# One gate pair moved from behind the attention into the head, attention scores and turned weights in separate PSUM places, and three more places for FFN rows

## The chip, the core and the metric

The kernel runs on one core of one Trainium2 chip. The metric is the device time of one execution in microseconds; the time before is the median of three runs, 1458.77 us (1458.38 to 1460.04). The core's engines are TensorE (PE; its weight loads are shown apart as PEld), VectorE (DVE), ScalarE (ACT), GpSimd (POOL) and SyncE (SP). Here POOL and SP mostly issue DMAs, and POOL does a few copies and memsets.

## The reference

One layer of a streaming encoder, over 1024 frames of a new stream and 64 frames of a running one; all in float32, with D_MODEL 1024, 8 heads of 64, CONV_DIM 512, D_FF 2816:

```python
def mixer(xn, conv_prefix, attn_fn, w_in, w_conv, w_conv_out, w_attn_out, w_out):
    proj = xn @ w_in
    cb, cc, ch, q, k, v, ga, gb = jnp.split(proj, splits, axis=-1)
    cv, conv_state = causal_conv(cc * ch, conv_prefix, w_conv)
    ya = (cb * cv) @ w_conv_out
    o, new_k, new_v = attn_fn(heads(q), heads(k), heads(v))
    yb = o.reshape(B, L, ATT_DIM) @ w_attn_out
    merged = jax.nn.sigmoid(ga) * ya + jax.nn.sigmoid(gb) * yb
    return merged @ w_out, conv_state, new_k, new_v

def swiglu(x, w1, w3, w2):
    return (jax.nn.silu(x @ w1) * (x @ w3)) @ w2

x = x + mixer(rmsnorm(x, g_mix), ...)
x = x + swiglu(rmsnorm(x, g_ffn), w_ff1, w_ff3, w_ff2)
return rmsnorm(x, g_final)
```

The attention is banded: a frame sees its own chunk of 64 and the eight before it, with a learned bias by clipped distance. `ga` and `gb` are 1024 channels each, the two gates.

## The kernel before

**Numbers.** Every product is made of three matmuls: a float32 operand is split into a high part (a cast on ACT) and a low part (a subtraction on DVE; `split`, lines 128 and 129), and high x high, high x low and low x high are added up in PSUM. Columns are the 1088 frames, in two halves of 544 (HT), each in two pieces of 272 (HN).

**The head.** Most columns of w_in go through `Unit` and `run`, one unit for 256 output channels: a 2 x 2 Strassen scheme with seven products instead of eight, each of 4 blocks x 3 matmuls x 2 pieces = 24 matmuls of 272 columns (line 280). `units` (line 540) is the order: q, k, cc, ch, cb, three of ga, and then four ya units (the product with w_conv_out, half as deep: 12 matmuls a product). A ga unit takes the sigmoid and stores its rows in DRAM (`a_done`); `gated_load` loads the rows of unit u into free parts of the scratch tile while an earlier unit runs, and `ya_done` multiplies them into the ya rows and stores these in `y_d`. The fourth ya unit has no gate unit in the head and stores its rows bare. The forms of the ya operand are written by `uforms` during the last unit ahead of ya.

**The gates outside the head.** Gates are 128-channel rows. The eight gb rows and the two ga rows 6 and 7 are plain products (`product`, lines 346 to 348): 4 pieces, each of 8 blocks x 3 = 24 matmuls. `plan` is the order of their weights, `prep` loads and splits them ahead, `next_w` hands them out; four pairs fit. The `x21` loads bring back the quarter of the normalised input whose place the Strassen forms took, which the pieces 2 and 3 of each gate need.

**The attention.** `attention` is a generator with 75 turns for 8 heads x 9 query tiles (t = 0 to 7 of the prompt with 1 to 5 key blocks of 128, and t = 8 for the sample): scores of step i, `softmax` (DVE adds the bias and takes the maximum, ACT takes exp and the sum), the transposes of step i - 2 with a `split` of the turned weights out of PSUM, and the value product of each pair of tiles one step later. Scores and turned weights share the PSUM pool `patt`, two buffers of two banks each, one tag. With the gates' three banks (`pmm`) and one for values (`ppv`) that is all eight banks. `between` lets PER = 3.15 turns run after each gate piece. The order: pieces 0 and 1 of four gates, then their pieces 2 and 3 and the other gates with attention turns behind each piece; ahead of the last LAST = 2 gates (ga 6 and 7) the attention is finished, and the tiles for the merge are made. The tile framework fixes the order on each engine when the program is built, by priority (order in the code) and by its own idea of when operands are ready.

**The merge.** For each row m in MERGE the yb product (lines 346 to 348, in `psum2`), z = sigmoid(gb) and t = the ya row are merged by DVE. `rows_in` loads gb and ya rows from DRAM. Rows 6 and 7 of ya are multiplied by their ga rows first (line 1189).

**The FFN.** The up products of 256 hidden channels are again Strassen units, (`a`, `b`) for w_ff1 and w_ff3. `hidden_done` forms seven combinations of a hidden row's halves and `keep` splits each into a row place and stores it in `h_d` (POOL, line 1458). There are three places: one in `hp` (hq) and two in `early` (hq_early). From the third pair on, part of the products is made jointly; `joint_forms` prepares operands for it in three tiles tj5, tj6, tj7 (first as tw6, tw7) of the pool `l2p`. The down product ends the kernel.

Of the kernel before, what the change touches and what calls it, by code (L numbers as in the profile page):

```python
# [8 lines left out]
F32 = mybir.dt.float32  # L9
# [6 lines left out]
P = 128  # L16
# [19 lines left out]
C_CB, C_CC, C_CH, C_Q, C_K, C_V, C_GA, C_GB = 0, 512, 1024, 1536, 2048, 2560, 3072, 4096  # L36
PER = 3.15
LAST = 2
# [28 lines left out]
def encoder_kernel(ctx: ExitStack, tc: tile.TileContext, ins, outs):  # L67
# [265 lines left out]
    def next_w():  # L333
        i = used[0]
        used[0] += 1
        prep(4 if i == 3 else i + 2)
        return plan[i]
# [13 lines left out]
    MERGE = [6, 7, 0, 1, 2, 3, 4, 5]  # L351
    GATES = [("b", m) for m in MERGE] + [("a", m) for m in range(6, 8)]
    for g, m in GATES:
        if m % 2 == 0:
            base = (C_GA if g == "a" else C_GB) + m * P
            ld = {"src": w_in[:, base : base + 2 * P], "w": 2 * P}
        plan.append((ld, KD, m % 2 * P))
# [183 lines left out]
    for nm, u in (  # L541
        ("q", 0), ("q", 1), ("k", 0), ("k", 1), ("cc", 0), ("ch", 0), ("ga", 0), ("cb", 0), ("cc", 1), ("ch", 1),
        ("ga", 1), ("cb", 1), ("ga", 2),
    ):
        base = {"q": C_Q, "k": C_K, "cc": C_CC, "ch": C_CH, "cb": C_CB, "ga": C_GA}[nm]
        units.append((nm, u, w_in[:, base + 2 * u * P : base + 2 * (u + 1) * P]))
# [167 lines left out]
    def ya_done(u):  # L714
        def f(r, h, src, snap):
            if u == 3:
                s = summed(src, snap, "ya")
            else:
                g = gated.pop((u, r, h))
                if snap is None:  # L720
                    s = snap1(None, "ya")
                    two = [t.rearrange("p (j n) -> p j n", j=2) for t in (s, g)]
                    vec.tensor_tensor(two[0], src, two[1], op=ALU.mult)
                else:
                    s = summed(src, snap)
                    vec.tensor_tensor(s, s, g, op=ALU.mult)
            nc.gpsimd.dma_start(row_of(y_d, u, r, h), s)

        return f
# [114 lines left out]
    for n in range(len(units)):  # L844
# [8 lines left out]
        else:  # L853
# [10 lines left out]
            unit = nxt_unit  # L864
        if n >= 12 and n < 15:
            gated_load(n - 12)
        if n == 13:
            x21_load(2)
        if n == 14:
            plain_load(0)  # L870
        for _ in r:
            if n == 12:
                uforms(si)
            if n < 2 and si in (2 + n, 5 + n):
                i = 2 * n + si // 5
                cache_tile(i)
                if i + 2 < 4:
                    cache_load(i + 2)
            if si > 1:
                for f in due:  # L880
                    f()
                due.clear()
            due += late
            late.clear()
            si += 1
# [15 lines left out]
    def gate(i, cs):  # L901
        g, m = GATES[i]
        for c in cs:
# [3 lines left out]
            if i >= len(GATES) - LAST:  # L907
                gate_out[0] = act.activation(ga_rows[m - 6][:, o : o + n], ps[:, :n], AF.Sigmoid).ins
                continue
# [89 lines left out]
    def scores(h, t):  # L999
        q, k, ks, v, vs, bias = heads[h]  # L1000
        ps = patt.tile([P, 2, 512], F32, tag="att", name=f"s{h}_{t}")
        s = at_pool.tile([P, 640], F32, tag="s", name=f"p{h}_{t}", bufs=4)
# [25 lines left out]
    def transposed(h, t, s):  # L1028
        tp = patt.tile([P, 2, 512], F32, tag="att", name=f"t{h}_{t}").rearrange("p a b -> p (a b)")
        if t == 8:  # L1030
            pt = pts_one
            for i in range(4):
                nc.tensor.transpose(
                    tp[:, i * TS : (i + 1) * TS], s[:TS, i * P : (i + 1) * P], ident[:TS, :TS]
                )
            nc.tensor.transpose(tp[:TS, 512 : 512 + TS], s[:TS, 512:576], ident[:TS, :TS])
            split(pt[:, 0, :4, :], pt[:, 1, :4, :], tp[:, : 4 * TS].rearrange("p (b t) -> p b t", t=TS))
            split(pt[:TS, 0, 4, :], pt[:TS, 1, 4, :], tp[:TS, 512 : 512 + TS])
            pts[h, 4] = pt

            sm = sums.pop(h)
            vec.reciprocal(sm, sm)
            tr = patt.tile([P, 2, 512], F32, tag="att", name=f"rt{h}")[:9, 0, :P]
            nc.tensor.transpose(tr, sm, ident)
# [14 lines left out]
        b0 = t - nb + 1 - max(0, 2 * g - 4)  # L1059
        for i in range(nb):  # L1060
            nc.tensor.transpose(tp[:, i * P : (i + 1) * P], s[:, i * P : (i + 1) * P], ident)  # L1061
        src = tp[:, : nb * P].rearrange("p (b t) -> p b t", t=P)
        js = slice(j * P, (j + 1) * P)
        split(pt[:, 0, b0 : b0 + nb, js], pt[:, 1, b0 : b0 + nb, js], src)

# [77 lines left out]
    def rows_in(m):  # L1143
        t, z = rows[m] = u_rows.tile([P, T], F32, tag="yg", name=f"yg{m}"), row_tile((MERGE.index(m) % 5 + 1) % 2, f"gb{m}")
        nc.sync.dma_start(z, gb_d[m * P : (m + 1) * P])
        nc.sync.dma_start(t, y_d[m * P : (m + 1) * P])
# [3 lines left out]
    x21_load(0)  # L1150
    for i in range(4):
        gate_w[i] = next_w()
        gate(i, (0, 1))
    for i in range(4):
        for c in (2, 3):
            gate(i, (c,))
            between()
        if i == 0:
            prep(5)
    for i in range(4, len(GATES)):  # L1160
        gate_w[i] = next_w()
        if i == len(GATES) - LAST:
# [7 lines left out]
            u_rows = pg_stack.enter_context(tc.tile_pool(name="u_rows", bufs=5, reuse_waits="tile"))  # L1170
            ga_rows = [uo.tile([P, T], F32, name=f"ga{m}") for m in (6, 7)]
            for k in range(2):
# [10 lines left out]
        for c in range(4):  # L1183
            gate(i, (c,))
            between()
        if i >= len(GATES) - LAST:
            m = GATES[i][1]
            t = rows[m][0]
            vec.tensor_tensor(t, t, ga_rows[m - 6], op=ALU.mult)


# [4 lines left out]
    for n, m in enumerate(MERGE):  # L1196
# [3 lines left out]
        t, z = rows.pop(m)  # L1200
        with tc.issue_after(gate_out[0]):
            act.activation(z, z, AF.Sigmoid)
        late = t.rearrange("p (h n) -> p h n", h=2)[:, :, 512:]
# [236 lines left out]
    def hidden_done(p):  # L1440
# [4 lines left out]
        def keep(c, x):  # L1445
# [3 lines left out]
            else:  # L1449
                n, kept_rows[0] = kept_rows[0] % 3, kept_rows[0] + 1  # L1450
                if n:
                    if kept_rows[1] is None:
                        kept_rows[1] = early.tile([P, 2, 4, 2, P], F32R, tag="raw", name="hq_early")
                    hq = kept_rows[1][:, n - 1]
                else:
                    hq = hp.tile([P, 4, 2, P], F32R, tag="hq", name=f"hq{p}_{c}", bufs=1)
# [206 lines left out]
    with tc.issue_after(urgent[0]), tc.issue_after(urgent[1]):  # L1663
# [4 lines left out]
        wp_stack.close()  # L1668
        hp = ctx.enter_context(tc.tile_pool(name="hp", bufs=2, reuse_waits="tile"))
    with tc.issue_after(newest[0]):  # L1670
        next(r0)
# [28 lines left out]
    def joint_forms():  # L1700
        l2p = up_stack.enter_context(tc.tile_pool(name="l2p", bufs=1, reuse_waits="tile"))

        def at(q, dtype, nm):
            return l2p.tile([P, 2, 2, HN], dtype, tag=f"tj{q}", name=nm)

# [422 lines left out]
```

## Time and profile before

| | us |
|---|---|
| median of three runs | 1458.77 (1458.38 to 1460.04) |
| the profiled execution | 1459.0 |
| its span, first to last instruction | 1456.9 |
| TensorE's granted clock, mean | 0.998 |

The page gives the busy time of each engine over the span; matmuls overlap and their ends are modelled, so the distance of one matmul's start from the next says more than the busy share. The stages by time: 0 to 66 norm and values of the head, 66 to 344 the Strassen units, 344 to 385 ya, 385 to 412 gate pieces alone, 412 to 590 the attention, 590 to 611 the last gates, 611 to 659 yb and merge, then the output product and the second norm, the FFN's up products from 787 on, the down product from about 1220 to the end.

### The profile page before, as it was taken

To read this page: it belongs to the slowest core of one execution; us is meant where nothing else is said; L and a number is where in the kernel's file an instruction comes from. 1 tells how busy PE (TensorE), PEld (TensorE's weight loads), DVE (VectorE), ACT (ScalarE), POOL (GpSimd) and SP (SyncE) were. 2 spreads that over 40 slices of the span, in tenths; PEclk is the share of its full clock that TensorE was granted. 3 is DMA by queue.
4 is the path that set the end of the run, shared out by engine and by line. 5 is a ranking of instruction groups with operands and counts; after the bars stand their busy time and mean duration, and the time that the engine had idled before them with its cause. 6 is when DMAs were issued, how large, how long until landed. Compare 5 with 4: busy or idle time off the path is not lost.

```text
span 1456.9 us, 26281 instructions
## 1 busy us (share of the span) xinstructions
PE 1441.3 (99%) x10083; PEld 1354.3 (93%) x10083; DVE 1033.4 (71%) x1939; ACT 693.3 (48%) x1389; POOL 156.2 (11%) x292
## 2 busy tenths in 40 slices
PE   8999999999999999999999999999999999999997
PEld 6899999999999989998889999999999998888886
DVE  7975565658457777572589787777777788857677
ACT  7654343436357667531456445454444455513223
POOL 1400010000211121111000111111011111000000
PEclk9999999999999999999999999999999999999999
DMA  8586512225878675843432444443344459767676
GB/s 284 184 281 224 192 63 74 66 102 198 251 218 213 171 191 149 294 150 117 152 112 75 155 169 144 155 149 130 136 143 162 164 201 324 251 230 246 214 266 208
DMA packets 156221, 262.48 MB, mean 180 GB/s; under 512 B 18528, under 2 KB 89376, under 8 KB 156096
## 3 DMA queue, kind: packets, MB, share of 16 engines
q1 hardware_dynamic: 132336, 184.33, 40.0%
q0 software_dynamic: 22608, 74.38, 14.2%
q10 hardware_dynamic: 1152, 2.10, 0.4%
q8 instruction: 79, 1.29, 0.4%
q14 instruction: 46, 0.38, 0.1%
HBM read 171.78 MB, written 90.81 MB: 180 GB/s over the span
## 4 chain that ended last, share of the span: by engine, by line
PE 87%; issue 8%; DVE 2%; ACT 1%; DMA 1%; POOL 1%; SPq 0%; ACTq 0%; POOLq 0%; DVEq 0%
PE A L2038 8%; PE Ab L1848 7%; PE Aa L1848 7%; PE D L2038 4%; PE Db L1848 4%; PE Da L1848 4%; PE J L1859 3%; PE g L347 3%; PE g L348 3%; PE g L346 3%; PE Aga L280 2%; PE B L2038 2%; PE t L1061 2%; PE Ak L280 2%; PE Aq L280 2%
## 5 line engine op out<-in xcount | busy, mean ns | idle before, releaser
L346 PE MATMUL g<-xn,wp 128*128 128x272 f32 x320 | 93.9, 294 | 0.0
L347 PE MATMUL g<-xn,wp 128*128 128x272 f32 x320 | 93.0, 291 | 0.0
L348 PE MATMUL g<-xn,low 128*128 128x272 f32 x320 | 92.9, 290 | 0.0
L128 ACT CAST ring<-w2r 128x512 fp32r<-128x512 f32 (+1 forms) x78 | 43.2, 587 | 96.0 <-PE A L2038 49.3
L972 DVE CUSTOM_DVE_ANT_0 p<-s,bb 128x640 f32<-128x640 f32 (+5 forms) x72 | 47.6, 662 | 38.5 <-PE s L1015 36.9
L2038 PE MATMUL A<-ring,low 128*128 128x512 f32 (+1 forms) x270 | 72.6, 384 | 0.0
L2038 PE MATMUL A<-ring,ht 128*128 128x512 f32 (+1 forms) x267 | 72.4, 387 | 0.0
L346 PEld LDWEIGHTS g<-xn,wp 128*128 128x128 f32 x320 | 60.3, 188 | 0.6
L347 PEld LDWEIGHTS g<-xn,wp 128*128 128x128 f32 x320 | 60.3, 188 | 0.4
L348 PEld LDWEIGHTS g<-xn,low 128*128 128x128 f32 x320 | 60.2, 188 | 0.4
L128 ACT CAST wa<-rawa 128x512 fp32r<-128x512 f32 x46 | 28.4, 621 | 66.2 <-PE Db L1848 20.9
L2038 PEld LDWEIGHTS A<-ring,low 128*128 128x128 f32 x270 | 50.1, 188 | 10.2 <-DVE acc L2053 0.2
L2038 PEld LDWEIGHTS A<-ring,ht 128*128 128x128 f32 x267 | 49.8, 188 | 10.2
L982 ACT ACTIVATE p<-p,mx 128x640 f32<-128x640 f32 (+5 forms) x72 | 50.8, 706 | 13.9 <-DVE mx L972 13.5
L129 DVE TENSOR_TENSOR ring<-w2r,ring 128x512 fp32r<-128x512 f32 (+1 forms) x78 | 48.7, 648 | 9.5 <-ACT ring L128 9.3
L129 DVE TENSOR_TENSOR pt<-t,pt 128x640 fp32r<-128x640 f32 (+2 forms) x64 | 41.8, 653 | 15.6 <-ACT pt L128 14.7
L1259 PE MATMUL wo<-low,mg 128*128 128x512 f32 x128 | 50.9, 397 | 0.0
L1261 PE MATMUL wo<-wo,mg 128*128 128x512 f32 x128 | 50.1, 391 | 0.0
L1260 PE MATMUL wo<-low,mg 128*128 128x512 f32 x128 | 49.9, 390 | 0.0
L129 DVE TENSOR_TENSOR low<-rawa,wa 128x512 fp32r<-128x512 f32 x46 | 30.8, 688 | 26.0 <-ACT wa L128 26.0
L1458 POOL DMA_DIRECT2D h_d<-hq_early x46 | 24.8, 538 | 225.2 <-DVE hq_early L129 215.2
L1848 PE MATMUL Ab<-mg,wb 128*128 128x272 f32 x288 | 47.4, 286 | 0.0
(671 smaller groups left out, 4642.0 us busy)
## 6 DMA issues: line engine op xcount, KB each, us to landing
h_d<-hq_early POOLq DMA_DIRECT2D x46, 512.0 KB, 3.6
ht<-h_d SPq DMA_DIRECT2D x77, 256.0 KB, 3.7
low<-h_d SPq DMA_DIRECT2D x77, 256.0 KB, 3.9
h_d<-hq POOLq DMA_DIRECT2D x24, 512.0 KB, 3.1
rawa<-in_w_ff SPq DMA_DIRECT2D x11, 1024.0 KB, 5.4
rawb<-in_w_ff SPq DMA_DIRECT2D x11, 1024.0 KB, 5.4
w2r<-in_w_ff SPq DMA_DIRECT2D x11, 1024.0 KB, 6.3
qd<-q_d SPq DMA_DIRECT2D x32, 272.0 KB, 4.2
```

Of the source, the lines that this page charges most:

```text
L128: a = act.copy(hi, src)
L129: b = vec.tensor_tensor(lo, src, hi.bitcast(F32), op=ALU.subtract)
L280: newest[0] = mm(t[:, j, :HN], w[:, k, :], x[p][:, k, l, j * HN : (j + 1) * HN], start=p in (1, 2, 7) and k == 0 and n == 0, stop=k == las ...
L346: mm(out, a, first, start=k == 0, stop=False)
L347: mm(out, a, then, start=False, stop=False)
L348: newest[0] = mm(out, b, p, start=False, stop=k == kt - 1).ins
L982: act.activation(s, s, AF.Exp, bias=mx, scale=-1.0, accum_out=sm)
L1259: mm(ps, x(k, 0), wh, start=f, stop=False)
L1260: mm(ps, x(k, 1), wh, start=False, stop=False)
L1261: mm(ps, x(k, 0), wl, start=False, stop=e)
L1848: mm(t[:, j, :HN], w[:, k, :], x[:, k, l, j * HN : (j + 1) * HN], start=p in (1, 7) and k == 0 and n == 0, stop=k == 3 and n == 2, skip_gr ...
L2038: mm(t[:, c], ht[k][:, j, x], w[:, l, c], start=p in (1, 2, 7) and k == 0 and n == 0, stop=k == len(ks) - 1 and n == 2, skip_group_check=p ...
```

## The change

Four parts:

1. `units` gets a fourth ga unit (ga3). All ya units are then gated; `gated_load`, `x21_load(2)`, `plain_load(0)` and `uforms` move one unit later. `GATES` is only the eight gb rows.
2. Only two gates run their first two pieces ahead of the attention instead of four; PER goes from 3.15 to 3.75. Six gb rows lie ahead of the attention's end, and the last two (gb 4 and 5) behind it, with their sigmoid written straight to SBUF tiles (`gb_late`), so that these rows are neither stored nor loaded again, and take no sigmoid in the merge. The multiplications by ga behind the attention go.
3. In `patt` scores have the tag "s" with one buffer of two banks, turned weights the tag "t" with two buffers of one bank. With four or five blocks a turned tile is made in two parts (three blocks, then the rest), each with its own bank and its own `split`. The sample's five blocks fit one bank.
4. `keep` puts the fourth to sixth row into the tiles of the tags tj7, tj6 and tj5, whose pool is opened earlier.

```diff
-PER = 3.15
+PER = 3.75
@@ next_w
-        prep(4 if i == 3 else i + 2)
+        prep(i + 2)
@@
-    GATES = [("b", m) for m in MERGE] + [("a", m) for m in range(6, 8)]
+    GATES = MERGE
@@ units
-        ("ga", 1), ("cb", 1), ("ga", 2),
+        ("ga", 1), ("cb", 1), ("ga", 2), ("ga", 3),
@@ ya_done
-            if u == 3:
-                s = summed(src, snap, "ya")
...
+            g = gated.pop((u, r, h))
+            if snap is None:
+                s = snap1(None, "ya")
+                two = [t.rearrange("p (j n) -> p j n", j=2) for t in (s, g)]
+                vec.tensor_tensor(two[0], src, two[1], op=ALU.mult)
             else:
...
+                s = summed(src, snap)
+                vec.tensor_tensor(s, s, g, op=ALU.mult)
@@
-        if n >= 12 and n < 15:
-            gated_load(n - 12)
-        if n == 13:
+        if 13 <= n < 17:
+            gated_load(n - 13)
+        if n == 14:
             x21_load(2)
-        if n == 14:
+        if n == 15:
             plain_load(0)
@@ gate
-                gate_out[0] = act.activation(ga_rows[m - 6][:, o : o + n], ps[:, :n], AF.Sigmoid).ins
+                gate_out[0] = act.activation(gb_late[m][:, o : o + n], ps[:, :n], AF.Sigmoid).ins
@@ scores
-        ps = patt.tile([P, 2, 512], F32, tag="att", name=f"s{h}_{t}")
+        ps = patt.tile([P, 2, 512], F32, tag="s", name=f"s{h}_{t}", bufs=1)
@@ transposed
-        tp = patt.tile([P, 2, 512], F32, tag="att", name=f"t{h}_{t}").rearrange("p a b -> p (a b)")
+        def bank(nm):
+            return patt.tile([P, 512], F32, tag="t", name=nm)
...
-        for i in range(nb):
-            nc.tensor.transpose(tp[:, i * P : (i + 1) * P], s[:, i * P : (i + 1) * P], ident)
-        src = tp[:, : nb * P].rearrange("p (b t) -> p b t", t=P)
...
-        split(pt[:, 0, b0 : b0 + nb, js], pt[:, 1, b0 : b0 + nb, js], src)
+        for a, b in ((0, nb),) if nb < 4 else ((0, 3), (3, nb)):
+            tp = bank(f"t{h}_{t}_{a}")
+            for i in range(a, b):
+                nc.tensor.transpose(tp[:, (i - a) * P : (i - a + 1) * P], s[:, i * P : (i + 1) * P], ident)
+            src = tp[:, : (b - a) * P].rearrange("p (b t) -> p b t", t=P)
+            split(pt[:, 0, b0 + a : b0 + b, js], pt[:, 1, b0 + a : b0 + b, js], src)
@@ rows_in
+        if m in gb_late:
+            z = gb_late[m]
+        else:
...
@@ order of the gates
-    for i in range(4):
+    for i in range(2):
         gate_w[i] = next_w()
         gate(i, (0, 1))
-    for i in range(4):
+    for i in range(2):
         for c in (2, 3):
             gate(i, (c,))
             between()
-        if i == 0:
-            prep(5)
-    for i in range(4, len(GATES)):
+    for i in range(2, len(GATES)):
...
-        if i >= len(GATES) - LAST:
-            m = GATES[i][1]
-            t = rows[m][0]
-            vec.tensor_tensor(t, t, ga_rows[m - 6], op=ALU.mult)
@@ merge
-        with tc.issue_after(gate_out[0]):
-            act.activation(z, z, AF.Sigmoid)
+        if m not in gb_late:
+            with tc.issue_after(gate_out[0]):
+                act.activation(z, z, AF.Sigmoid)
@@ keep
-                n, kept_rows[0] = kept_rows[0] % 3, kept_rows[0] + 1
-                if n:
+                n, kept_rows[0] = kept_rows[0], kept_rows[0] + 1
+                first = 2 < n < 6
+                n %= 3
+                if first:
+                    t = small.tile([P, 4 * HN], F32R, tag=f"tj{7 - n}", name=f"hq_tj{n}")[:, :1024]
+                    hq = t.rearrange("p (i l t) -> p i l t", i=4, l=2)
+                elif n:
```

More of the change, by code (lines that the diff above doesn't have):

```diff
@@ L351, in encoder_kernel @@
     MERGE = [6, 7, 0, 1, 2, 3, 4, 5]
-    GATES = [("b", m) for m in MERGE] + [("a", m) for m in range(6, 8)]
-    for g, m in GATES:
+    GATES = MERGE
+    for m in GATES:
         if m % 2 == 0:
-            base = (C_GA if g == "a" else C_GB) + m * P
+            base = C_GB + m * P
             ld = {"src": w_in[:, base : base + 2 * P], "w": 2 * P}
@@ L715, in f @@
         def f(r, h, src, snap):
-            if u == 3:
-                s = summed(src, snap, "ya")
-            else:
[L719 to L726, printed above, removed]
+            g = gated.pop((u, r, h))
[3 more added lines that the diff above has]
+                vec.tensor_tensor(two[0], src, two[1], op=ALU.mult)
+            else:
+                s = summed(src, snap)
+                vec.tensor_tensor(s, s, g, op=ALU.mult)
             nc.gpsimd.dma_start(row_of(y_d, u, r, h), s)
@@ L864, in encoder_kernel @@
             unit = nxt_unit
[L865 to L867 removed]
+        if 13 <= n < 17:
+            gated_load(n - 13)
+        if n == 14:
             x21_load(2)
[L869 removed]
+        if n == 15:
             plain_load(0)
         for _ in r:
[L872 removed]
+            if n == 13:
                 uforms(si)
@@ L901, in gate @@
     def gate(i, cs):
-        g, m = GATES[i]
+        m = GATES[i]
         for c in cs:
@@ L1028, in transposed @@
     def transposed(h, t, s):
-        tp = patt.tile([P, 2, 512], F32, tag="att", name=f"t{h}_{t}").rearrange("p a b -> p (a b)")
+        def bank(nm):
+            return patt.tile([P, 512], F32, tag="t", name=nm)
         if t == 8:
+            tp = bank(f"t{h}_{t}")
             pt = pts_one
@@ L1035, in transposed @@
                 )
-            nc.tensor.transpose(tp[:TS, 512 : 512 + TS], s[:TS, 512:576], ident[:TS, :TS])
+            nc.tensor.transpose(tp[:TS, 4 * TS : 5 * TS], s[:TS, 512:576], ident[:TS, :TS])
             split(pt[:, 0, :4, :], pt[:, 1, :4, :], tp[:, : 4 * TS].rearrange("p (b t) -> p b t", t=TS))
-            split(pt[:TS, 0, 4, :], pt[:TS, 1, 4, :], tp[:TS, 512 : 512 + TS])
+            split(pt[:TS, 0, 4, :], pt[:TS, 1, 4, :], tp[:TS, 4 * TS : 5 * TS])
             pts[h, 4] = pt
@@ L1042, in transposed @@
             vec.reciprocal(sm, sm)
-            tr = patt.tile([P, 2, 512], F32, tag="att", name=f"rt{h}")[:9, 0, :P]
+            tr = bank(f"rt{h}")[:9, :P]
             nc.tensor.transpose(tr, sm, ident)
@@ L1143, in rows_in @@
     def rows_in(m):
-        t, z = rows[m] = u_rows.tile([P, T], F32, tag="yg", name=f"yg{m}"), row_tile((MERGE.index(m) % 5 + 1) % 2, f"gb{m}")
-        nc.sync.dma_start(z, gb_d[m * P : (m + 1) * P])
+        t = u_rows.tile([P, T], F32, tag="yg", name=f"yg{m}")
+        if m in gb_late:
+            z = gb_late[m]
+        else:
+            z = row_tile((MERGE.index(m) % 5 + 1) % 2, f"gb{m}")
+            nc.sync.dma_start(z, gb_d[m * P : (m + 1) * P])
+        rows[m] = t, z
         nc.sync.dma_start(t, y_d[m * P : (m + 1) * P])
@@ L1170, in encoder_kernel @@
             u_rows = pg_stack.enter_context(tc.tile_pool(name="u_rows", bufs=5, reuse_waits="tile"))
-            ga_rows = [uo.tile([P, T], F32, name=f"ga{m}") for m in (6, 7)]
+            gb_late = {m: uo.tile([P, T], F32, name=f"gbl{m}") for m in GATES[-LAST:]}
             for k in range(2):
@@ L1669, in encoder_kernel @@
         hp = ctx.enter_context(tc.tile_pool(name="hp", bufs=2, reuse_waits="tile"))
+        small = up_stack.enter_context(tc.tile_pool(name="l2p", bufs=1, reuse_waits="tile"))
     with tc.issue_after(newest[0]):
@@ L1700, in joint_forms @@
     def joint_forms():
-        l2p = up_stack.enter_context(tc.tile_pool(name="l2p", bufs=1, reuse_waits="tile"))
         def at(q, dtype, nm):
-            return l2p.tile([P, 2, 2, HN], dtype, tag=f"tj{q}", name=nm)
+            return small.tile([P, 2, 2, HN], dtype, tag=f"tj{q}", name=nm)
         def whole(o, k, j):
```

## The prediction

> **What bounds the kernel now.** I read the page's first two parts first, then busy time by stage, then the chain of waits, then the attention's engines by shape.
>
> ```profile
> span 1456.9 us, 26281 instructions
> PE 1441.3 (99%) x10083; PEld 1354.3 (93%) x10083; DVE 1033.4 (71%) x1939; ACT 693.3 (48%) x1389; POOL 156.2 (11%) x292
> PEclk9999999999999999999999999999999999999999
> ```
>
> TensorE is busy for 99% at full clock, but these ends are modelled, so I count starts. The stages, with columns PE, weight load, DVE, ACT, POOL, clock, DMA share, GB/s:
>
> ```profile
> 344.00:385.00 41.00, 41.00 (x334) 40.89 (x332) 33.22 (x67) 19.50 (x42) 7.86 (x15) 1.00 0.69 229
> 385.00:400.00 15.00, 15.00 (x123) 15.00 (x122) 0.73 (x2) 2.63 (x6) 3.96 (x14) 1.00 1.01 300
> 400.00:412.00 12.00, 12.00 (x99) 12.00 (x98) 0.00 (x0) 1.55 (x4) 2.17 (x4) 1.00 0.89 275
> 412.00:590.00 178.00, 176.21 (x1276) 163.16 (x1276) 129.52 (x327) 125.70 (x313) 34.22 (x67) 1.00 0.69 184
> 800.00:860.00 60.00, 58.60 (x472) 58.17 (x472) 49.80 (x88) 29.43 (x56) 9.91 (x19) 1.00 0.42 151
> ```
>
> The first is the four ya units, the next two are gate pieces alone while DMA is full and DVE empty, the fourth is the attention with gate pieces between its steps, the last is the start of the FFN. In all of them TensorE ends last, so a matmul fewer is time, and so is a hole filled. From the chain of waits and the timeline:
>
> ```profile
> 204.42 2.96 PE Aga L280 x24
> 385.00 0.29 PE L346 MATMUL g<-xn,wp 128*128 128x272 f32 x1
> 411.95 0.22 PE L1014 MATMUL s<-kd,qd 128*128 128x128 f32 x1
> 589.67 0.34 PE L346 MATMUL g<-xn,wp 128*128 128x272 f32 x1
> ```
>
> A Strassen product of 24 matmuls takes 2.96 us. From the first gate matmul to the first score are 26.95 us, in which the code has nine pieces (two of each of four gates, then one): 2.99 a piece. The attention runs from 411.95 to 589.67, 177.7 us for 72 steps and 24 pieces; behind it 7 pieces more.
>
> **The change part by part.** *A gate pair into the head.* It takes away gates a6 and a7 as plain products, 8 pieces x 2.99 = 23.9 us, and adds unit ga3, 7 products x 2.96 = 20.7 us: **-3.2 us**. No dependency is needed for this, and the other ga units run in the chain without a gap (2.96 after 2.96). What comes with it: one weight load of 1 MB for one that goes; four stores and four loads of ga rows, 1.1 MB each way, on SP; two gb rows fewer stored by POOL (8 pieces) and fewer loaded by SP (2 rows). The gate loads of the last ya unit stand on SP ahead of the next gate weights and of the attention's first loads; they wait for ya unit 1 to give its places back, 20 us before those are wanted, so I cost them at nothing. DVE gets four multiplications in the last ya unit and loses two behind the attention:
>
> ```profile
> L726 DVE TENSOR_TENSOR scr<-scr 128x544 f32<-128x544 f32 x9 | 6.5, 720 | 0.0
> L1189 DVE TENSOR_TENSOR yg<-yg,ga 128x1088 f32<-128x1088 f32 x2 | 2.6, 1286 | 0.0
> ```
>
> 4 x 0.72 = 2.9 us on a DVE that is busy 33.2 of 41 us there. TensorE's 41 us of products cover it; without that cover it would cost 2.9. The two that go (2.6 us) and two sigmoids over 1088 columns lie under products of the stage behind the attention: nothing.
>
> *Fewer pieces around the attention.* Before its first step stand five pieces instead of nine; between steps 19 or 20 instead of 24. As matmuls these are counted above. As cover they are the doubtful part. What the first step needs, from the timeline and from the views of the tiles kd and bb (which give issue to landing as least, median, most):
>
> ```profile
> 398.17 1.49 SPq L953 DMA_DIRECT2D kd<-k_d  x2
> DMA to landing us min/median/max: 5.5/5.9/11.2
> 404.60 0.59 SPq L937 DMA_DIRECT2D bb<-bias_d  x1
> DMA to landing us min/median/max: 2.6/3.9/6.3
> ```
>
> The second of the last key loads is issued at about 399.2 and lands at 404.7 at the earliest, 19.7 us after ya's end; the bias at 407.2, 22.2 after. Today the first score stands at 26.95, behind both. After the change it may stand at 5 x 2.99 = 14.95. Bounds: nothing, if the order of matmuls, which is fixed when the program is built, puts two or three more pieces ahead of it (pieces with split weights are there); 22.2 - 14.95 = 7.3 us if it does not. I take nothing: wherever the attention waits today, gate matmuls stand in the gap. Both ends go into the range.
>
> *Own PSUM places.* Scores and turned weights shared a ring of two double banks; scores now have one double bank, turned weights two single ones, filled and copied in two parts when there are four or five blocks. A heavy stretch today:
>
> ```profile
> 531.77 0.74 PE L1061 MATMUL t<-ident,p 128*128 128x128 f32 x5
> 532.27 1.07 PE L1085 MATMUL pv<-pt,vd 128*128 128x512 f32 x4
> 532.60 0.69 ACT L128 CAST pt<-t 128x640 fp32r<-128x640 f32 x1 [0.81 <-PE t L1061]
> 533.18 0.31 PE L1014 MATMUL s<-kd,qd 128*128 128x320 f32 x1
> 533.33 0.82 DVE L129 TENSOR_TENSOR pt<-t,pt 128x640 fp32r<-128x640 f32 x1 [0.78 <-ACT pt L128]
> 533.75 0.29 PE L347 MATMUL g<-xn,wp 128*128 128x272 f32 x1
> 534.21 0.77 PE L1061 MATMUL t<-ident,p 128*128 128x128 f32 x5
> ```
>
> Transposes, cast, subtraction (ends 534.15), next transposes at 534.21: a ring of one, 2.44 us a step. TensorE's own part of such a step, from the starts: transposes 0.50, scores 0.57, and half of a value product, which every second step has (0.91 with four matmuls, six in the later pairs): 1.5 to 1.7 us. 24 pieces over 75 steps add 0.96: 2.5 to 2.7, just over the ring's 2.44. With 20 pieces (0.80) it is 2.3 to 2.5, and the old ring would have become the bound; that is what the split takes away, so with it I expect no new hole from this side. What it costs is instructions on ACT and DVE:
>
> ```profile
> L129 DVE TENSOR_TENSOR pt<-t,pt 128x640 fp32r<-128x640 f32 x32 | 26.4, 823 | 11.1 <-ACT pt L128 10.6
> L129 DVE TENSOR_TENSOR pt<-t,pt 128x512 fp32r<-128x512 f32 x8 | 5.4, 679 | 0.5 <-ACT pt L128 0.5
> L129 DVE TENSOR_TENSOR pt<-t,pt 128x384 fp32r<-128x384 f32 x8 | 4.5, 557 | 1.7 <-ACT pt L128 1.4
> L129 DVE TENSOR_TENSOR pt<-t,pt 128x256 fp32r<-128x256 f32 x8 | 3.3, 416 | 0.4 <-ACT pt L128 0.4
> L129 DVE TENSOR_TENSOR pt<-t,pt 128x128 fp32r<-128x128 f32 x8 | 2.2, 279 | 1.9 <-ACT pt L128 1.9
> L972 DVE CUSTOM_DVE_ANT_0 p<-s,bb 128x640 f32<-128x640 f32 x32 | 26.2, 820 | 5.3 <-PE s L1015 4.9
> L972 DVE DVE_READ_ACCUMULATOR2_ANT mx<- 128x1 f32 x64 | 5.2, 81 | 0.0
> L990 DVE TENSOR_TENSOR co<-pv,ca 64x256 f32<-64x256 f32 x32 | 13.2, 413 | 0.6
> L129 DVE TENSOR_TENSOR low<-rawp,wp 128x512 fp32r<-128x512 f32 x20 | 13.7, 687 | 5.8 <-ACT ga L908 3.1 <-ACT wp L128 2.5
> ```
>
> 32 x (557 + 416 - 823) + 8 x (557 + 279 - 679) ns = 6.1 us more on DVE, less 4 weight splits of 0.69 that two gates no longer need: 129.5 + 6.1 - 2.7 = 133 us in a window of 177.7 - 4 x 2.99 = 165.7: 80% against 73% now. ACT's casts grow by about as much from a lower base. I take the attention's holes as they are: **0**. Bounds, by what the window holds beyond its matmuls: 24 pieces are 72 us of the 177.7; by the starts above a transpose takes 0.10, a score matmul 0.14, a value matmul 0.23, and by the calls in the code that is 24 (240 transposes) + 18 (128) + 22 (96) + 5 (48 of half the width); the small matmuls of the short steps, some 180, I estimate at 0.12 like the gate's, 22. That leaves some 14 us of holes, none long. Half of them gained or half as much again lost: -7 to +7.
>
> *Three FFN row places.* The view of waits has one long hole of TensorE behind the attention; the timeline shows what stood ahead of it on ACT:
>
> ```profile
> PE Aa L280 <- ACT sa_Q L267: 1.3, 1, 1.3
> 813.30 0.62 ACT L128 CAST hq_early<-sa 128x512 fp32r<-128x512 f32 x1 [2.03 <-DMA h_d<-hq_early]
> 816.59 0.62 ACT L128 CAST hq<-sa 128x512 fp32r<-128x512 f32 x1 [2.67 <-DMA h_d<-hq]
> 817.67 0.59 ACT L267 COPY sa_Q<-Aa 128x544 f32<-128x544 f32 x1
> ```
>
> The copy that frees the PSUM bank stands on ACT behind a cast that waits for its row place to be stored. With three more places the fourth to sixth row need no old place, and the seventh finds one stored long ago. The copy can follow the product's end at about 813.9 within 2 us, before TensorE, busy with the next product until 816.8, wants the bank: **-1.3 us**. What may be late next: the places are those of the joint forms, of which DVE makes six instructions before 799 today; they now wait for the stores of three rows (about 816) and fall into 815 to 861, where the first is read. DVE has about ten idle microseconds there for 4.3 us of work: nothing, at worst the 1.3 again.
>
> Sum: -3.2 - 1.3 = -4.5 us on the profiled execution's own 1459.0 us (span 1456.9), which lies 0.2 above the median 1458.77 of the runs: **1454.5 us**.
>
> **The rivals.** *A, the first head comes late (slower).* The first score stands right behind the fifth piece, and TensorE waits there for keys (4.7 us) or bias (7.3). It decides once fewer than two pieces follow the fifth ahead of the scores. For it: DMA share 1.01 in just these microseconds. Against: spare pieces exist. 1459.2 to 1461.8, at its far end 3 us slower than before.
>
> *B, DVE becomes the attention's bound.* A heavy step costs it 0.82 + 0.08 for the scores, 0.56 + 0.42 for the turned weights and two additions of 0.41 in every second step: 2.3 us, and weight splits on top, against TensorE's 2.3 to 2.5 with 20 pieces. For it: 0.15 us more a step than today with less cover. Against: light steps leave DVE time. Ten to twenty hundredths late on 32 heavy steps: +3 to +6, 1457.5 to 1460.5. [...]
>
> *C, the rings were the holes.* If the ring of 2.44 us made them, half of the 14 us goes with it, 7 us, or a quarter: 1447.5 to 1451. For it: the transposes at 534.21 start 0.06 us behind the subtraction. Against: the waits that the view names for them are 1.1 us in all.
>
> *D, a part does nothing:* the FFN's 1.3 us stay, 1455.8; within the forecast's own range.
>
> **How the numbers follow.** Forecast (with D) 0.50, own range 1452.5 to 1457; A 0.20; B 0.15; C 0.15. The range 1450 to 1461 leaves out the ends of A and C. About 0.2% (2.9 us) is what a measurement of this kernel can tell from no change. Faster than 1455.9: four fifths of the forecast and C, 0.56. Slower than 1461.7: A's far end and what I have not seen, 0.11. Between: 0.33.
>
> **What would show it.** The last ya matmul ends 20.7 us later, at 405.7; right if the first score follows without a hole, A if DVE or DMA ends a wait of TensorE there. Scores to the last value product: 166 us is the forecast, 170 or more is B, 162 or less is C. The FFN's wait for sa_Q is gone. From gates to the end of the yb products nothing else moves: the latter end 3.2 us earlier, near 655.5. I am wrong if the head has holes, or if the attention's length changes by more than the pieces taken out.

## The result, and the profile after: 22.6 us slower

The changed kernel takes 1482.05 us (median of four runs, 1480.90 to 1482.92), the kernel before 1459.40 us on the same chip: ratio 1.0156, 95% interval 1.0144 to 1.0167. The forecast was 1454.5, the range ended at 1461. The profiled execution took 1480.9 us. Its page, first lines and TensorE's clock:

```profile
span 1479.0 us, 26339 instructions
...
PE 1448.5 (98%) x10059; PEld 1357.9 (92%) x10059; DVE 1042.7 (71%) x1991; ACT 699.2 (47%) x1429; POOL 150.3 (10%) x283
...
PEclk9999999999999999999999999999999999999999
```

No engine has become a bound, and the page's clock row (slices of 37 us) shows nothing. The view of TensorE's waits does (what it waited for: us in total, times, longest):

```profile
PE s L1011 <- DVE mx L969: 6.9, 8, 3.3
PE g L346 <- ACT gbl L905: 4.3, 1, 4.3
PE s L1011 <- DMA kd<-k_d: 3.4, 1, 3.4
```

In the kernel before the first of these was 0.6 us and the other two were absent. The wait for sa_Q in the FFN, 1.3 us, is gone as forecast. Where the new waits lie, in TensorE's timeline (start, duration, what it is, idle before and what ended it):

```profile
405.55 0.29 PE L346 MATMUL g<-xn,wp 128*128 128x272 f32 x1
...
425.85 0.30 PE L1011 MATMUL s<-kd,qd 128*128 128x128 f32 x1 [3.41 <-DMA kd<-k_d]
...
612.39 0.74 PE L1074 MATMUL pv<-pts,vsd 128*128 128x128 f32 x5 [0.91 <-issue]
617.40 0.59 PE L346 MATMUL g<-xn,wp 128*128 128x272 f32 x1 [4.27 <-ACT gbl L905]
...
634.06 0.29 PE L346 MATMUL yb<-ob,wp 128*128 128x272 f32 x1
...
682.14 0.39 PE L1260 MATMUL wo<-low,mg 128*128 128x512 f32 x1
```

The first gate matmul stands 20.55 us later than before (405.55 against 385.00; forecast 20.7). The time is lost behind it. From the first gate to the first matmul of the output product (wo) it is 276.6 us, against 273.7 before, where that matmul stood here:

```profile
658.74 0.39 PE L1259 MATMUL wo<-low,mg 128*128 128x512 f32 x1
```

Eight pieces of 2.99 us are gone from this stretch, so it should have been 249.8. **26.8 us are lost between these two marks**, and they are nearly the whole miss (27.2 us by the medians, 1482.05 against 1459.40 - 4.5). I use this stretch as the measure below. By windows (PE, weight load, DVE, ACT, POOL, clock, DMA share, GB/s):

```profile
420.00:440.00 20.00, 16.54 (x110) 15.49 (x109) 7.31 (x21) 9.87 (x24) 1.63 (x3) 0.91 0.92 255
440.00:560.00 120.00, 115.30 (x801) 103.06 (x800) 88.28 (x249) 85.87 (x236) 21.33 (x42) 1.00 0.66 167
560.00:590.00 30.00, 26.54 (x168) 24.28 (x167) 17.03 (x50) 16.48 (x46) 5.38 (x11) 0.89 0.61 156
...
612.00:640.00 28.00, 23.34 (x173) 23.23 (x174) 13.37 (x17) 15.67 (x24) 2.98 (x5) 0.88 0.87 324
```

Three stretches have holes and a lower clock: the first head, a border between heads, the end of the attention. The border was the surprise. SP's queue and DVE there, one timeline view for each engine:

```profile
555.60 0.45 SPq L951 DMA_DIRECT2D ksd<-k_d  x1
...
559.29 0.59 SPq L933 DMA_DIRECT2D bb<-bias_d  x1
559.93 0.59 SPq L934 DMA_DIRECT2D bb<-bias_d  x1
```

```profile
566.04 0.29 DVE L969 CUSTOM_DVE_ANT_0 p<-s,bb 128x128 f32<-128x128 f32 x1 [4.56 <-DMA bb<-bias_d]
```

```profile
566.39 0.58 PE L1011 MATMUL s<-kd,qd 128*128 128x256 f32 x1 [3.27 <-DVE mx L969]
```

DVE's first reduction of a head adds the bias, and the bias (bb) has just been issued, behind the loads of the sample's keys (ksd), which have one place and wait until the head before has used it (4.0 us by the view of SP's waits). TensorE cannot go on with the second score tile, since the first still lies in the only score place. In the kernel before, the same view of SP has them ten microseconds the other way round, and DVE's reduction never waited for bb:

```profile
550.73 0.59 SPq L937 DMA_DIRECT2D bb<-bias_d  x1
...
560.49 0.56 SPq L954 DMA_DIRECT2D ksd<-k_d  x1
```

In the changed kernel, the view of line 969's instructions (DVE sat idle before them until: us, times) has

```profile
  DMA bb<-bias_d: 11.2, 5
```

Nothing in the change names these loads.

### The profile page after: what moved, and what is told of

The parts are those of the page before. It is cut to its first block, busy times and chain, and to the rows that moved or that the text cites. A ratio compares the mean times of both kernels' runs of the same rounds, so it can differ in the third digit from the quotient of the medians.

```text
span 1479.0 us, 26339 instructions
## 1 busy us (share of the span) xinstructions
PE 1448.5 (98%) x10059; PEld 1357.9 (92%) x10059; DVE 1042.7 (71%) x1991; ACT 699.2 (47%) x1429; POOL 150.3 (10%) x283
## 4 chain that ended last, share of the span: by engine, by line
PE 91%; DMA 3%; DVE 3%; ACT 2%; SPq 1%; issue 1%; ACTq 0%; DVEq 0%
PE A L2043 8%; PE Ab L1853 7%; PE Aa L1853 7%; PE D L2043 4%; PE Db L1853 4%; PE Da L1853 4%; PE J L1864 3%; PE Aga L280 3%; PE B L2043 2%; PE wo L1260 2%; PE wo L1262 2%; PE wo L1261 2%; PE t L1064 2%; PE Ak L280 2%; PE Aq L280 2%; PE Acc L280 2%
## 5 line engine op out<-in xcount | busy, mean ns | idle before, releaser
L346 PE MATMUL g<-xn,wp 128*128 128x272 f32 x256 | 76.6, 299 | 4.3 <-ACT gbl L905 4.3
L347 PE MATMUL g<-xn,wp 128*128 128x272 f32 x256 | 77.1, 301 | 0.0
L348 PE MATMUL g<-xn,low 128*128 128x272 f32 x256 | 76.5, 299 | 0.0
L969 DVE CUSTOM_DVE_ANT_0 p<-s,bb 128x640 f32<-128x640 f32 (+5 forms) x72 | 47.6, 662 | 27.2 <-PE s L1012 14.4
L129 DVE TENSOR_TENSOR ring<-w2r,ring 128x512 fp32r<-128x512 f32 (+1 forms) x78 | 48.6, 645 | 10.3 <-ACT ring L128 10.0
L346 PEld LDWEIGHTS g<-xn,wp 128*128 128x128 f32 x256 | 50.0, 195 | 5.2 <-ACT gbl L905 4.4
L129 DVE TENSOR_TENSOR pt<-t,pt 128x384 fp32r<-128x384 f32 (+2 forms) x104 | 46.7, 458 | 7.8 <-ACT pt L128 6.7
L348 PEld LDWEIGHTS g<-xn,low 128*128 128x128 f32 x256 | 49.9, 195 | 0.4
L347 PEld LDWEIGHTS g<-xn,wp 128*128 128x128 f32 x256 | 49.9, 195 | 0.2
L128 ACT CAST pt<-t 128x384 fp32r<-128x384 f32 (+2 forms) x104 | 40.5, 406 | 15.6 <-PE t L1064 13.9
L2058 DVE TENSOR_TENSOR acc<-A,acc 128x512 f32<-128x512 f32 x51 | 34.6, 684 | 18.3 <-PE A L2043 18.3
```

Of the source, the lines that this page charges most:

```text
L128: a = act.copy(hi, src)
L129: b = vec.tensor_tensor(lo, src, hi.bitcast(F32), op=ALU.subtract)
L346: mm(out, a, first, start=k == 0, stop=False)
L347: mm(out, a, then, start=False, stop=False)
L348: newest[0] = mm(out, b, p, start=False, stop=k == kt - 1).ins
```

## The experiments

The theory from these views: the gate pieces taken out were cover (work that TensorE can do while another operand is still on its way), not only work, and their number also shaped the order in which the program was built, the DMA issues' order included. The rival: the split PSUM ring did it, with one score place and more instructions on ACT and DVE. All results, with the stretch from the first gate to the output product in the profiled run:

| kernel | median, us | ratio to before, 95% interval | gates to output product, us |
|---|---|---|---|
| before | 1459.40 | | 273.7 |
| changed | 1482.05 | 1.0156 (1.0144 to 1.0167) | 276.6 |
| e1_ffn | 1457.45 | 0.9990 (0.9980 to 0.9999) | |
| e2_psum | 1458.42 | 0.9993 (0.9984 to 1.0003) | 273.5 |
| e3_gates | 1475.58 | 1.0112 (1.0095 to 1.0129) | 268.4 |
| e4_bias | 1466.71 | 1.0051 (1.0036 to 1.0066) | 261.1 |
| e5_start | 1465.27 | 1.0043 (1.0028 to 1.0058) | 260.4 |
| e6_store | 1465.20 | 1.0036 (1.0024 to 1.0048) | 261.3 |
| e6_behind | 1469.67 | 1.0080 (1.0056 to 1.0104) | 262.2 |
| e7_ks | 1472.88 | 1.0098 (1.0083 to 1.0114) | 271.2 |
| e8_store | 1462.00 | 1.0021 (1.0011 to 1.0030) | 256.5 |
| e9_ring | 1467.88 | 1.0053 (1.0038 to 1.0068) | 263.8 |
| e10_cover | 1479.83 | 1.0140 (1.0125 to 1.0155) | 273.4 |
| e11_late | 1466.26 | 1.0047 (1.0030 to 1.0064) | 280.5 |
| e12_per | 1463.70 | 1.0030 (1.0020 to 1.0040) | 258.2 |
| e13_six | 1464.37 | 1.0038 (1.0023 to 1.0053) | 259.4 |
| e14_34 | 1457.90 | 0.9991 (0.9983 to 1.0000) | |

The ratio is to the kernel before, run beside each kernel on the same chip; the first row is the one that ran beside the changed kernel. Where there are holes, runs of one kernel spread by up to 9 us (e6_behind 1466.4 to 1475.7), so the stretch, from a single profiled run, is uncertain by a few microseconds there.

### The parts alone

e1_ffn: the kernel before with the last part of the change only.

```diff
+                if first:
+                    t = small.tile([P, 4 * HN], F32R, tag=f"tj{7 - n}", name=f"hq_tj{n}")[:, :1024]
...
+        small = up_stack.enter_context(tc.tile_pool(name="l2p", bufs=1, reuse_waits="tile"))
```

> The kernel before with the FFN row places alone. Both theories: the term of the prediction stands, -1.3 us (1457 to 1458.5), the wait of TensorE for sa_Q gone. If this part had cost something unseen, 1460 or more.

Measured 1457.45, 1.4 us below the kernel before on that chip; the wait for sa_Q is gone. That term was right.

e2_psum: the kernel before with the split ring only.

```diff
+        ps = patt.tile([P, 2, 512], F32, tag="s", name=f"s{h}_{t}", bufs=1)
...
+            return patt.tile([P, 512], F32, tag="t", name=nm)
```

> The kernel before with the split of the PSUM ring alone (gates and their pieces as before, nine pieces ahead of the attention, 24 in it). Theory 1, that the missing gate pieces did the harm: 1456 to 1461, the attention 174 to 180 us. Theory 2, that the one place for scores and the added casts and subtractions did it: 1470 to 1480, the attention 188 us or more, TensorE waiting for the reduction of the scores before.

1458.42, from the first score to the last value product 177.2 us against 177.6. The rival theory falls: with all 40 pieces in place the split costs nothing that can be measured, and gains nothing.

e3_gates: the changed kernel with the ring of the kernel before.

> The changed kernel with the old shared PSUM ring and whole transposes (the gates, their pieces and the FFN row places as changed). Theory 1 (fewer pieces as cover): still 1473 to 1485, with a late first head and a hole behind the attention. Theory 2 (PSUM split): 1453 to 1460.

1475.58: the gates alone do most of it. It is 6.5 us less than the whole change, though. Its built order has the bias late for some heads only, so this isn't a clean measure of the split.

### The bias

e4_bias moves one call in `head_load`.

```diff
     def head_load(h):
+        if h:
+            bias_load(h)
         q = []
...
-        if h:
-            bias_load(h)
```

> The changed kernel with one move: for heads 1 to 7 the four bias loads are issued ahead of the head's other loads instead of behind them. Theory 1a, that the late bias makes the holes at the heads' borders (about 7 to 9 us of the 13.9 by which the attention grew): 1472 to 1476, the waits for the reduction (6.9 us, 8 times) down to under 2. Theory 1b, that the borders wait for something else (the keys of the sample, the single score place): 1480 to 1484, unchanged.

1466.71: **15.3 us from four DMA issues a head**, twice what I had read off the holes. The wait for the reduction is down from 6.9 to 0.4 us. What I hadn't counted are the slow matmuls behind the longest hole (some 3 us, shown at the end of this document), and 14 gate matmuls that had been drawn forward into the attention (514 there, 500 here) and were missing behind it, 1.7 us. A few microseconds more stay open.

e7_ks leaves the bias where it is and takes away what it queued behind.

```diff
-        ks = hd_pool.tile([P, CACHE + TS], F32R, tag="ks", name=f"ksd{h}", bufs=1)
+        ks = hd_pool.tile([P, CACHE + TS], F32R, tag="ks", name=f"ksd{h}", bufs=2)
```

> The changed kernel with a second place for the keys of the sample (their loads no longer wait for the head before to end), the bias loads where the change has them. If the bias is late because its issues stand on SP behind the waiting loads of those keys, it lands early here too and the holes at the heads' borders go: 1465 to 1470, as with the early bias. If the bias's own place in the queue or its DMA time makes it late, 1478 to 1484.

1472.88, between the two cases. The wait of line 969 for the bias is gone here too, and the wait for the reduction is 0.7 us, so the queue was the cause; but only 9.2 us come back. Its order still differs: the hole behind the attention came back larger (two waits for gbl, 6.4 us).

e11_late turns it round: the kernel before with the split ring and all 40 pieces, and the bias held behind the sample's keys.

```diff
+            with tc.issue_after(last_ks):
+                bias_load(h)
```

> The kernel before with the split PSUM ring, and the bias loads of heads 1 to 7 held behind the loads of the sample's keys on SP, where the change has them; all 40 gate pieces stay. If the late bias costs by itself, whatever the cover: 1468 to 1475 (the 9 to 15 us that the early bias gave back). If 24 pieces in the attention cover it: 1458 to 1461.

1466.26, again between the two cases. The first wait in the view of TensorE's waits:

```profile
PE s L1015 <- DVE mx L973: 5.2, 7, 1.6
```

The late bias costs 7.8 us against e2_psum even with 24 pieces in the attention, less than the 9 to 15 of the first case and far from nothing: about half of what it costs the changed kernel.

### The start and the end

e5_start, on top of e4_bias, puts the third pair of gate weights behind the first head's loads.

```diff
-            if step in (1, 3, 5):
+            if step in (1, 3):
...
+            if i == 4:
+                with tc.issue_after(first_head[0]):
+                    nc.sync.dma_start(raw, src)
```

> The changed kernel with the early bias loads, and the load of the third pair of gate weights (1 MB) issued behind the first head's loads instead of ahead of them. If the hole ahead of the first score (2.9 us, and the slow matmuls behind it, 1.6) is the time that the last keys take to land, they land about 3.3 us sooner (1 MB at 300 GB/s) and the kernel takes 1461.5 to 1464. If the DMA queues are held by something else there (latency, not bytes), 1465 to 1468 as with the early bias alone.

The keys land sooner (in e4_bias the DMAs moved 303 GB/s from 406 to 420 us), the first score stands at 421.27, 15.0 us behind the first gate matmul, without a hole: the mechanism is right. Yet the time, 1465.27, is only 1.4 us less than that of e4_bias (the intervals overlap), in the range of the other case. The gain has been given back in a hole behind the attention:

```profile
PE g L351 <- ACT gbl L910: 4.3, 1, 4.3
```

That hole, in the changed kernel itself, on ACT:

```profile
613.17 0.21 ACT L985 COPY ca_s<-pv 64x64 f32<-64x64 f32 x1 [1.78 <-PE pv L1074]
613.54 2.10 ACT L128 CAST ob<-o 128x1088 fp32r<-128x1088 f32 x2 [0.16 <-issue]
615.66 1.28 ACT L905 ACT_TABLE_LOAD   x1
616.95 0.97 ACT L905 ACTIVATE gbl<-g 128x272 f32<-128x272 f32 x3
```

The last two gates leave PSUM by a sigmoid into tiles made behind the attention. Where the built order draws three of their pieces ahead of the last value product, all three gate banks are full, and TensorE waits for two casts and a table load. The kernel before has the same row of ACT work, but 168 gate matmuls (seven pieces) still to come at that point and free banks; here it is 120.

e6_store, on top of e4_bias, stores these two gates like the others; e6_behind holds their products behind the last value product.

```diff
-            if i >= len(GATES) - LAST:
-                gate_out[0] = act.activation(gb_late[m][:, o : o + n], ps[:, :n], AF.Sigmoid).ins
-                continue
...
+            gate_out[0] = act.copy(st[:, :n], ps[:, :n]).ins
```

> The changed kernel with the early bias loads, and the last two gates stored to HBM through the staging tiles like the six others, and loaded back with the other rows, instead of being turned by ACT into tiles of the pool that opens behind the attention. If the hole behind the attention (2.5 us, and slow matmuls behind it, near 2) is the wait of these products' PSUM banks for that pool and for ACT, it goes: 1462 to 1464.5. If the rows that are loaded back come late for the last yb products, or the cover was missing anyway, 1466 or more.

```diff
+            if i >= len(GATES) - LAST:
+                with tc.issue_after(att_end[0]):
+                    product(ps[:, :n], gate_w[i], xn, o, n)
...
```

> The changed kernel with the early bias loads, and the last two gates' products held behind the last value product on TensorE (32 pieces, eight of them behind the attention). They then cover ACT's work behind the attention, as in the kernel before, but no gate matmul is left in the attention's last steps. If the attention's end can stand without them: 1462 to 1464. If the cover is simply too little, the holes move into the last steps (transposes and value products waiting for ACT and DVE) and it takes 1466 to 1470.

e6_store: 1465.20, between the two cases; the wait for gbl is gone, the yb products start 2.1 us earlier than in e4_bias, and take 2.5 us longer, waiting for DVE. e6_behind: 1469.67, no better; no wait behind the attention, but these in its last steps (timeline of TensorE):

```profile
587.40 0.71 PE L1091 MATMUL pv<-pt,vd 128*128 128x512 f32 x2 [1.08 <-DVE co L991]
...
591.05 0.46 PE L1037 MATMUL t<-ident,p 64*128 64x64 f32 x4 [1.36 <-DVE pt L129]
...
595.08 0.74 PE L1078 MATMUL pv<-pts,vsd 128*128 128x128 f32 x5 [2.03 <-issue]
```

A hole filled in one place opens in another.

### All three repairs, and what is left

e8_store joins the edits of e4_bias, e5_start and e6_store.

> The changed kernel with all three repairs: early bias loads, the third weight pair behind the first head's loads, the last two gates stored and loaded back. If the three holes are independent: first score near 421, no hole of TensorE over 1 us up to the first yb product, 1458 to 1461. If the cover is what is short, one hole filled opens another (as the start's gain came back behind the attention): 1463 to 1466.

1462.00, just behind the upper edge of the first case: 20 of the 22.6 us are back. From gates to yb it is now 203.0 us, where 225.7 - 23.9 = 201.8 was forecast. The rest is in the yb stage, 53.4 us against 48.1, where only 92 gate matmuls stand ahead of it and its operand isn't ready:

```profile
PE yb L352 <- DVE ob L129: 1.9, 2, 1.2
PE yb L351 <- ACT ob L128: 1.0, 1, 1.0
```

e9_ring is the same with the old ring.

> The same with the shared PSUM ring and whole transposes of the kernel before (so the gates, the FFN row places and the three repairs). If the split of the ring costs nothing when the bias is early: 1458 to 1461, as with it. If the single place for scores and the added casts cost with fewer gate pieces, it is 3 to 6 us faster than that: 1454 to 1457, below the kernel before. If the old ring was the bound with fewer pieces, as the prediction had it, it is slower: 1463 to 1468.

1467.88, 5.9 us slower. The sign is that of the third case, but most of it (4.6 us) is a longer yb stage, with fewer pieces left behind the attention (66 matmuls against 92), so it doesn't show that the ring itself was the bound.

Is the rest a matter of where the pieces stand? e13_six holds six of them behind the attention, e12_per spaces the steps otherwise.

```diff
+            if i == len(GATES) - 1 or i == len(GATES) - 2 and c > 1:
+                with tc.issue_after(att_end[0]):
...
```

> The three repairs, and six gate pieces (the last gate and half of the one before) held behind the last value product. With four there, TensorE waited some 3 us for the casts of the first yb products' data and ran slow behind that (6.1 us lost in all). If it is only where the pieces stand: 1456 to 1459. If 32 pieces are too few: those 6 us move into the attention's last steps, 1460 to 1465.

```diff
-PER = 3.75
+PER = 4.2
```

> The three repairs, with the steps of the attention handed out at 4.2 a piece instead of 3.75 (18 pieces among the steps, ten behind them in the code). If the spacing decides: 1457 to 1460, with fewer small gaps at the end. If the built order pulls the pieces forward again, as its matmul order suggests (under four pieces behind the last value product): 1461 to 1464, no change.

1464.37 and 1463.70. With six pieces behind, the yb stage is back at 48.6 us, and the attention's last steps have the holes of e6_behind. In e12_per the same 92 matmuls stand behind the attention as without it. Neither placing wins the rest.

e10_cover tests the theory as a whole: the changed kernel with the two gates computed a second time where the kernel before had them.

```diff
-    GATES = MERGE
+    GATES = [("b", m) for m in MERGE] + [("a", m) for m in range(6, 8)]
...
-    for i in range(2):
+    for i in range(4):
         gate_w[i] = next_w()
         gate(i, (0, 1))
...
```

> The changed kernel with the two gates a6 and a7 computed a second time around the attention, as in the kernel before, and not used there (40 pieces instead of 32, PER 3.15, four gates started ahead of the attention): 8 x 2.99 = 23.9 us of products more than the change. Theory (the pieces taken out were cover): the holes go with them, the time is that of the kernel before plus the Strassen unit less the FFN hole, 1458.9 + 20.7 - 1.4 = 1478.2, some 4 us faster than the change although it does more; the bias issues stand ahead of the sample's keys again. Rival (the unit in the head, its rows or its loads do the harm): the change plus 23.9, 1500 to 1506.

**1479.83: with 192 more matmuls, 23.9 us of products, it is no slower than the change** (2.2 us less, but the two intervals overlap). TensorE's windows (around the first head, the attention, behind it) have no long hole and full clock, and SP issues the bias ahead of the keys again, though no line says so:

```profile
407.00:434.00 27.00, 27.00 (x219) 27.00 (x218) 1.85 (x3) 3.47 (x10) 6.42 (x18) 1.00 0.96 288
434.00:611.00 177.00, 175.15 (x1271) 162.06 (x1271) 132.76 (x367) 128.75 (x352) 34.30 (x67) 1.00 0.68 186
611.00:632.00 21.00, 21.00 (x170) 21.00 (x170) 10.41 (x12) 9.93 (x16) 1.59 (x2) 1.00 0.82 283
```

```profile
550.20 0.59 SPq L934 DMA_DIRECT2D bb<-bias_d  x1
559.03 0.55 SPq L951 DMA_DIRECT2D ksd<-k_d  x1
```

The unit in the head, its loads and its stores cost 20.6 us net and, with the FFN's 1.4 added, 22.0; 20.7 was forecast. e10_cover differs from the change in the number of pieces, in PER, in the gates started ahead and in how the last ones leave PSUM; which of these moved the bias in the built order was not separated.

e14_34 is the change without its gates: the split ring and the row places.

> The kernel before with the split ring and the FFN row places together (all of the change but its gates). If the two add: 1457, 1 to 2 us under the kernel before. If the split takes back what the row places give: 1458.5 to 1459.5.

1457.90, ratio 0.9991 (0.9983 to 1.0000). With e1_ffn (1457.45) these are the only two whose interval does not reach above the kernel before; the gain, about 1.4 us, is less than 0.2%, and the FFN part alone has all of it.

## Why the prediction was wrong, step by step

- **The gate pair into the head, -3.2 us.** The unit's price was near enough (22.0 by e10_cover; the first gate 20.55 us later in the changed kernel). But the eight pieces did not give 23.9 us back. With the three repairs the stretch is some 17 us shorter than before (256.5 against 273.7), less than the unit costs: as this kernel stands, the swap itself loses.
- **"I take nothing: wherever the attention waits today, gate matmuls stand in the gap."** This is the step that failed. The pieces that stood in those gaps were the ones taken out. I put the term at 0, with a bound of +7.3 that I looked for at the first head alone; the stretch shows 26.8 us, at the start, at the borders of the heads and behind the attention. It is not cover alone. The late bias costs 7.8 us with all pieces in place (e11_late against e2_psum). Fewer pieces, with the gates' new places that come with them and the bias early, cost 12.3 us more than the sum had it (1466.71 against 1458.88 - 4.5, where 1458.88 is the kernel before on that chip). Both together cost 27.2, some 7 us more than the two apart, which fits that fewer pieces cover less of a late load. What made the program builder put the bias late was not shown.
- **The first head.** Rival A had the mechanism: the last keys let the first score go 20.3 us behind the first gate (19.7 was my earliest landing), and TensorE waited 3.4 us, in spite of 5.6 pieces ahead. Bias was not what ended it, and about 1.6 us more went with the slow matmuls behind. Alone it would have been about 5 us. That this lies inside A's 4.7 to 7.3 is luck: A put all of it down to the wait, which was shorter, and had no slow matmuls.
- **The bias of the later heads** stood in no rival. I had weighed the queue for the loads that the diff moves ("The gate loads of the last ya unit stand on SP ahead") and took the order of all others as given. It isn't: moving them ahead gave 15.3 us back, over half of the miss.
- **Behind the attention.** I counted "7 pieces more" there before and never asked how many would be left: five. The hole was 4.3 us, with about 1.7 more for the slow matmuls.
- **Own PSUM places, 0.** Right with all pieces in place (e2_psum); whether the old ring would have been the bound with fewer pieces stays open (e9_ring). B is out: DVE is busy 88.28 of 120 us in the attention's middle, 74%, and where TensorE waited for DVE's reduction (6.9 us) DVE itself had mostly waited for the bias; with the bias early 0.4 us are left. My sign for B, 170 us or more from the first score to the last value product, was too coarse: it is 187.0 us in the changed kernel, and B is not the reason. What I didn't see is that with a single score place a late operand of DVE stops TensorE at the second tile, as the border above shows. C, that the ring made the holes, is out with e2_psum as well.
- **FFN row places, -1.3.** Right: 1.4 measured, and the giving back did not come.

Of the rest, 7.5 us between 1462.0 and the forecast, 5.3 lie in the yb stage (53.4 against 48.1), by the waits shown for lack of pieces behind the attention; that is argued from the waits. That no other arrangement would win it was not shown, only that e12_per and e13_six did not.

## What to carry to other kernels

Work that fills another stage's waits must be costed twice when it is taken out: once as work, once as cover, and for the cover list every place where it stood (start, borders, end) with what would be waited for there. Where a framework fixes the order on the engines, compare the order of DMA issues before and after a change too: a load that waits for its place can hold up the loads queued behind it, as the sample's keys held up the bias here (a second place for them, in e7_ks, gave 9.2 us back). If adding the work back, unused, costs no time, then what was lost is cover or the order that came with it, not the price of the work.

## What the runs showed of the hardware

With each of its three holes of over 3 us the changed kernel shows a slow stretch, in which TensorE's clock was 0.50: 3.41 us long from 426.40 on, behind the hole of 3.41 us; 6.83 us from 566.35 on, at the end of the hole of 3.27 us; 6.83 us from 614.13 on, within and behind the hole of 4.27 us. TensorE's windows ahead of, at and behind the slow stretch at the first head:

```profile
422.15:425.85 3.70, 0.29 (x4) 0.10 (x2) 0.69 (x1) 0.57 (x1) 0.00 (x0) 1.00 0.98 298
425.85:429.81 3.96, 3.96 (x20) 3.96 (x21) 0.91 (x3) 0.90 (x2) 0.38 (x1) 0.57 0.84 240
429.81:433.00 3.19, 3.19 (x25) 3.07 (x25) 0.43 (x2) 2.06 (x4) 0.16 (x1) 1.00 1.04 285
```

The clock was 0.57 on average there, and gate matmuls started 0.226 us apart instead of 0.125 (426.41 to 429.58 for 14 of them): about 1.6 us lost on top of the hole. What makes the clock fall was not shown, only where it fell. A shorter hole was enough in some places: where the changed kernel waited 3.41 us for the keys, e4_bias waited 2.7 us and e6_behind 2.4 us, and the clock from the score on was 0.56 in the one and 1.00 in the other:

```profile
425.10:429.00 3.90, 3.82 (x18) 3.85 (x19) 0.66 (x2) 0.90 (x2) 0.12 (x1) 0.56 0.83 231
```

```profile
424.70:429.00 4.30, 4.24 (x34) 4.27 (x35) 0.92 (x3) 1.88 (x3) 0.54 (x1) 1.00 0.83 242
```

Over the profiled runs of the changed kernel and of the experiments up to e13_six, all ten holes of 3.1 us and more in this part of the kernel were followed by such a stretch, and five of the ten between 2.2 and 3.0 us.

By the counts that follow, where the hole lay decided here. In narrow windows the clock was 1.00 or 0.50; in this part of the kernel each slow stretch was 3.41 or 6.83 us long, and within one run they started whole multiples of 3.41 us apart (in the changed kernel at 426.40, 566.35 and 614.13). So I cut the ten runs that have such a stretch into windows of 3.41 us on that grid. In 19 windows TensorE was idle for more than 1.75 us by the modelled ends, and the next window was slow each time; of the 16 with 0.8 to 1.71 us of idle time only one, with 1.68, had a slow window behind it. Two windows of the changed kernel, each with the next one, show both cases (1.62 and 1.90 us idle):

```profile
450.30:453.71 3.41, 1.79 (x15) 1.56 (x13) 0.94 (x4) 0.76 (x2) 2.64 (x5) 1.00 0.92 286
453.71:457.12 3.41, 3.17 (x19) 2.68 (x20) 2.01 (x7) 2.24 (x9) 0.20 (x1) 1.00 0.61 133
610.72:614.13 3.41, 1.51 (x12) 1.17 (x10) 1.42 (x5) 1.17 (x3) 1.91 (x4) 1.00 0.84 244
614.13:617.54 3.41, 0.14 (x1) 0.14 (x1) 2.49 (x2) 3.38 (x6) 0.00 (x0) 0.50 0.29 82
```

About half a window of idle time was enough here, and the 2.4 us of e6_behind went free; split over two windows, a hole of that length can stay under 1.75 us in each. Why some stretches lasted two windows stays open. The dearest lies behind the border in the changed kernel, where TensorE was busy for 6.78 of 6.82 us:

```profile
566.35:573.17 6.82, 6.78 (x27) 6.29 (x28) 3.46 (x12) 4.03 (x13) 0.78 (x2) 0.50 0.44 114
```

By the usual distances of the same matmuls, the stretches cost 1.5 to 3.2 us each. So a hole of 3 us with such a stretch cost 4.5 to 6 us.
